# S5 operators on GpSimd in a fixed order, six output buffers, and the output phase's loads behind them

## The chip, the cores and the metric

The kernel runs on one core of one Trainium2 chip. The metric is device microseconds (us) of one execution. Before the change three runs took 2718.73, 2725.08 and 2727.89 us; their median is 2725.08 us.

The engines are named as the profile names them: PE (TensorE), DVE (VectorE), ACT (ScalarE), POOL (GpSimd) and SP (SyncE, which issues DMAs). Each engine works through its own queue in order. An instruction that waits holds up all that stands behind it in that queue, DMA issues among them.

## The reference

A trunk of two layers over a sequence of 1024 tokens of width 1024, in float32: a gated linear attention (GLA) layer, then an S5 layer. In each layer the normalised input goes through one wide projection, whose columns feed the sequence mixer (width 2048), a gate z (3072) and a query (1024) for a cross-attention into 256 memory rows.

```python
for i in range(DEPTH):
    h = rms_norm(x, norm_w[i])
    ...
        seq_out, z, xq = s5_branch(h, s5_w_in[j], s5_lam_re[j], ...)
    xa = memory_attention(xq, mem_n, xa_w_kv[i])
    y = jnp.concatenate([seq_out.astype(x.dtype), xa.astype(x.dtype)], axis=-1) * jax.nn.silu(z)
    x = x + y @ w_out[i]
return rms_norm(x, final_norm_w)
```

The S5 mixer splits the 2048 channels into 128 groups of 16, each with 64 complex states: x_t = A x_{t-1} + B u_t and y_t = Re(C x_t), then a GELU and a gated product with `w_glu`.

## The kernel before

All matrix products go through `gemm` (L86): every float32 weight tile is loaded by SP (`wr`, L78) and split into a high part `wh` (ACT, L69) and a low part `wl` (DVE, L70), and each product is made of three matmuls.

The S5 layer works in steps of 8 tokens. For that it builds three kinds of operator matrices from the parameters, for 16 blocks n of 8 groups each:

- *In-chunk operators* (`s5_operators`, L774 to L821) hold what a token contributes within its own 8 tokens. POOL makes the factors (L785 to L807), ACT copies some of them into `cz`, PE multiplies them (L811), DVE and ACT form a Toeplitz tile (L814, L815), ACT issues seven DMAs that shift it (L818), copies it (L820) and stores it as `tp` in DRAM (L821).
- *Input operators* (`s5_input_operators`, 32 of them) take tokens to states. POOL issues two loads for each, `ib` (L754) and `ipw` (L757), one operator ahead, computes with L767 to L770, and stores `rt` to DRAM (L771).
- *Output operators* (`s5_output_operators`, 32 of them) take states to tokens. POOL multiplies powers `pwo` (loaded once by SP, L719) with parameters `oc` (L728): first multiply L741, second L742, then L743, and the store of `od` to DRAM (L744).

Input and output operators share buffers `op` (three) and `opt` (one) of pool `ip1`. In `run()` the in-chunk operators are called between the output projections of the first layer, all input and output operators before `mem_attention` of the second layer (scores, softmax, product `ps_b` with the values, gate, y at L322, store of y by SP at L323; y has two buffers). Then `s5()` runs.

`s5()` has two parts of eight units. A unit projects `u` (weights `w_su`), stores it to DRAM (L870), loads it in another layout (`uu`, L872) and forms with `rt` the inputs of the states (L853 to L860). A recurrence on DVE (L883, L885, L887) then walks through the 128 steps, in two independent chains per part. The output phase loads per half unit `uq` (L896), `tp` (L898) and `ow` (L900, the stored output operator), copies states into `xg`, and multiplies (L908, L909).

The order of the instructions on each engine is not the order of the calls. The Tile framework's scheduler orders them by a timeline that it simulates, by data dependences and by when buffers come free. Where a pool is closed, a later pool takes over its memory, and the later tiles wait for the last use of the earlier ones. The tiles of `s5()` lie in part in memory of the operators' pool:

```python
tile.TileContext(nc, schedule_with_timeline_sim=True)
...
return ctx.enter_context(self.tc.tile_pool(name=name, bufs=bufs, reuse_waits="tile"))
```

Of the kernel before, what the change touches and what calls it, by code (L numbers as in the profile page):

```python
# [8 lines left out]
F32 = mybir.dt.float32  # L9
# [7 lines left out]
P = 128  # L17
HALF = 512
# [27 lines left out]
class Trunk:  # L46
# [675 lines left out]
    def s5_output_operators(self, pool, powers, ns):  # L722

        nc = self.nc

        def load(n):
            c = pool.tile([P, 2, 4, 16], F32, tag="oc", name="oc", bufs=3)
            nc.gpsimd.dma_start(c.rearrange("p r g h -> p (r g h)"), self.t["s5_par"][n][:, 128:256])  # L728
            return c

        sh = [P, 4, 8, 16]
        nxt = load(ns[0])
        for n in ns:
            c, nxt = nxt, load(n + 1) if n < ns[-1] else None
            pw = [powers[:, i, 4 * n:4 * n + 4].rearrange("p g (d o) -> p g d o", o=1).broadcast_to(sh) for i in range(2)]
            c = [c[:, i].rearrange("p g (o h) -> p g o h", o=1).broadcast_to(sh) for i in range(2)]
            od = self.o_d[n].rearrange("(r p) (i g) x -> r i p g x", r=2, i=2)
            for r, op in enumerate((ALU.subtract, ALU.add)):
                o = pool.tile([P, HALF], F32, tag="op", name="op", bufs=3).rearrange("p (g t h) -> p g t h", g=4, h=16)
                tm = pool.tile([P, HALF], F32, tag="opt", name="opt", bufs=1).rearrange("p (g t h) -> p g t h", g=4, h=16)  # L740
                nc.gpsimd.tensor_tensor(o, pw[0], c[r], ALU.mult)  # L741
                nc.gpsimd.tensor_tensor(tm, pw[1], c[1 - r], ALU.mult)  # L742
                nc.gpsimd.tensor_tensor(o, o, tm, op)  # L743
                nc.gpsimd.dma_start(od[r], o.rearrange("p g t h -> p g (t h)"))  # L744

    def s5_input_operators(self, pool):

# [25 lines left out]
    def s5_operators(self, pool, n):  # L773

        nc, t, v = self.nc, self.t, self.nc.vector
        M, A, S = ALU.mult, ALU.add, ALU.subtract
        gs = slice(4 * n, 4 * n + 4)
        G = 4
        par = pool.tile([P, 448], F32, tag="par", name="par", bufs=2)
        nc.gpsimd.dma_start(par, t["s5_par"][n])  # L780
        view = lambda a, b, pat, **kw: par[:, a:b].rearrange(pat, **kw)
        b = view(0, 128, "p (r g h) -> p r g h", r=2, g=G)
        c = view(128, 320, "p (r g h) -> p r g h", r=3, g=G)
        dd = view(320, 448, "p (i g h) -> p i g h", i=2, g=G)
        nc.gpsimd.tensor_scalar(par[:, 192:320], par[:, 192:320], -1.0, None, M)  # L785
        cz = self.cz[n % 2]
        halves = [slice(64 * i, 64 * i + 64) for i in range(2)]
        for i, hp in enumerate(halves):
            nc.scalar.copy(cz[hp, :, :, 0, i], c[hp, 0:2])
        c4 = pool.tile([P, 2, G, 16], F32, tag="c4", name="c4", bufs=2)  # L790
        l4 = [self.pw[:, i, gs, 4:5].broadcast_to([P, G, 16]) for i in range(2)]
        for i in range(2):
            tm = pool.tile([P, G, 16], F32, tag="ptm", name="ptm", bufs=1)
            nc.gpsimd.tensor_tensor(c4[:, i], l4[0], c[:, i], M)
            nc.gpsimd.tensor_tensor(tm, l4[1], c[:, i + 1], M)
            nc.gpsimd.tensor_tensor(c4[:, i], c4[:, i], tm, A)
        for i, hp in enumerate(halves):
            nc.scalar.copy(cz[hp, :, :, 1, i], c4[hp])
        r = pool.tile([P, 2, G, 4, 16], F32, tag="r", name="r", bufs=2)
        sh = [P, G, 4, 16]  # L800
        pw = [self.ip[:, i, 4:8, gs].rearrange("p s g -> p g s").rearrange("p g (s o) -> p g s o", o=1).broadcast_to(sh) for i in range(2)]
        xs = [b[:, i].rearrange("p g (o h) -> p g o h", o=1).broadcast_to(sh) for i in (0, 1, 1, 0)]
        for i, op in ((0, S), (1, A)):
            tm = pool.tile(sh, F32, tag="ctm", name="ctm", bufs=1)
            nc.gpsimd.tensor_tensor(r[:, i], pw[0], xs[2 * i], M)
            nc.gpsimd.tensor_tensor(tm, pw[1], xs[2 * i + 1], M)
            nc.gpsimd.tensor_tensor(r[:, i], r[:, i], tm, op)  # L807
        pk = self.ps("a")[0:64, :G * 64]
        for g in range(G):
            for ri in range(2):  # L810
                nc.tensor.matmul(pk[:, g * 64:(g + 1) * 64], r[:, ri, g].rearrange("p s h -> p (s h)"), cz[:, ri, g].rearrange("p e i h -> p (e i h)"), start=ri == 0, stop=ri == 1)  # L811
        pk = pk.rearrange("p (g e i h) -> p e i g h", g=G, e=2, i=2)
        tp = self.toep[n % 2]
        v.tensor_tensor(tp[64:P, 7], pk[:, 0], dd[0:64], A)  # L814
        nc.scalar.copy(tp[0:64, 7], pk[:, 1])  # L815
        for s in range(7):
            w = 16 * (s + 1)
            nc.scalar.dma_start(tp[0:w, s], tp[P - w:P, 7])  # L818
        tg = pool.tile([P, 8, 8, 16], F32, tag="tg", name="tg", bufs=1)
        nc.scalar.copy(tg, tp.rearrange("p t i g h -> p (i g) t h"))  # L820
        nc.scalar.dma_start(self.tp_d[n].rearrange("p a b -> p (a b)"), tg.rearrange("p a t h -> p (a t h)"))  # L821
# [15 lines left out]
    EARLY = 8  # L837

    def s5(self, xs, zs_d, y1_d):
        nc, t, v = self.nc, self.t, self.nc.vector  # L840
        ud = [self.dram.tile([8, P, P], F32, name=f"ud{j}") for j in range(16)]
        by_step = [x.rearrange("s (h g) c -> (s h) g c", g=8) for x in ud]
        with ExitStack() as ctx:
            st = [self.pool(ctx, f"st{i}").tile([P, 2, 32, P + 1], F32, name=f"st{i}") for i in range(2)]
            sp = self.tags(ctx, "s5")
            for part in range(2):
                nc.gpsimd.memset(st[part][:, :, :, 0:1], 0.0)
                def states(j, uu):
                    half, jl = divmod(j, 8)
                    hp = slice(64 * half, 64 * half + 64)  # L850
# [37 lines left out]
            for part in range(2):  # L888
                for j in self.PARTS[part]:
                    half, jl = divmod(j, 8)  # L890
                    hp = slice(64 * half, 64 * half + 64)
                    yo = sp.tile([P, 8, P], F32, tag="uy", name="uy", bufs=3)
                    for q in range(2):
                        n, hb = 2 * jl + q, slice(4 * half, 4 * half + 4)
                        uq = sp.tile([P, 4, P], F32, tag="uq", name="uq", bufs=2)
                        nc.sync.dma_start(uq, by_step[j][:, 4 * q:4 * q + 4, :])  # L896
                        tp = sp.tile([P, 4, P], F32, tag="rtp", name="rtp", bufs=3)
                        nc.sync.dma_start(tp, self.tp_d[n][:, hb, :])  # L898
                        ow = sp.tile([P, 4, P], F32, tag="ow", name="ow", bufs=2)
                        nc.sync.dma_start(ow, self.o_d[n][:, hb, :])  # L900
                        xg = sp.tile([P, 4, P], F32, tag="xg", name="xg", bufs=2)
                        g0 = 8 * (jl % 4) + 4 * q
                        nc.scalar.copy(xg[0:64], st[part][hp, 0, g0:g0 + 4, 0:P])
                        nc.vector.tensor_scalar(xg[64:P], st[part][hp, 1, g0:g0 + 4, 0:P], -1.0, None, ALU.mult)
                        ps = self.ps("a")
                        for g in range(4):
                            o = ps[:, g * P:(g + 1) * P]
                            nc.tensor.matmul(o, tp[:, g], uq[:, g], start=True, stop=False)  # L908
                            nc.tensor.matmul(o, ow[:, g], xg[:, g], start=False, stop=True)  # L909
                        nc.scalar.activation(yo[:, 4 * q:4 * q + 4, :], ps.rearrange("p (g c) -> p g c", g=4), AF.Gelu_apprx_tanh)  # L910
                    nc.sync.dma_start(y1_d[j].rearrange("s (h g) c -> (s h) g c", g=8), yo)
# [50 lines left out]
    def run(self):  # L962
        nc, tc, t = self.nc, self.tc, self.t
# [6 lines left out]
        with ExitStack() as ctx:  # L970
# [14 lines left out]
            with ExitStack() as c2:  # L985
# [12 lines left out]
                with ExitStack() as c3:  # L998
                    late, pool = self.pool(c3, "xl0"), self.pool(c3, "xa0")
# [41 lines left out]
            with ExitStack() as c2:  # L1041
                qp = self.pool(c2, "xq1")
                self.kvp = self.pool(c2, "kv1")
                late, pool = self.pool(c2, "xl1"), self.pool(c2, "xa1")
                ip = self.pool(c2, "ip1")
                self.s5_input_operators(ip)
                self.s5_output_operators(ip, self.s5_output_powers(ip), range(16))
                self.mem_attention(qp, late, pool, self.mem_kv_reload, t["w_sx"], [t["w_sz"][16 + i] for i in range(8)], xs1, y_d[1])
            self.s5(xs1, zs_d, y1_d)
            self.glu(xp, y1_d, zs_d, y_d[1])  # L1050
# [95 lines left out]
```

## Time and profile before

| | before |
|---|---|
| median of three runs | 2725.08 us |
| the profiled execution | 2727.05 us |
| its span in the trace | 2725.3 us |
| mean granted TensorE clock | 0.955 of full speed |
| PE busy | 2468.2 us (91%) |
| DVE busy | 1285.9 us (47%) |
| ACT busy | 834.0 us (31%) |
| POOL busy | 597.1 us (22%) |

The page cuts the span into 40 slices of 68 us. The row of PE has 9 in most of them, and 4, 5 and 0 in some of the slices between 1160 and 1700 us; POOL works from slice 14 to slice 24 and hardly anywhere else. The shares are means over stages that are limited by different things, so the stretches are read one by one. The profiled execution lies 2 us above the median.

### The profile page before, as it was taken

How to read it: one execution, taken by the hardware profiler on the slowest of the kernel's cores; microseconds unless marked ns; L12 is line 12 of the kernel's file. 1: busy time of each engine (PE TensorE's matmuls, PEld its weight loads, DVE VectorE, ACT ScalarE, POOL GpSimd, SP SyncE). 2: the span in 40 equal slices, each digit the busy share in tenths (PEclk: the TensorE clock that was granted, in tenths of full speed). 3: DMA queues.
4: the chain of work that ended last, by engine and by line, in shares of the span. 5: the costliest groups of instructions: out<-in, count | busy, mean ns of one | idle time of the engine just before them, and what ended most of it. 6: DMA issues, size and time to landing. Idle time of an engine off the chain costs nothing.

```text
span 2725.3 us, 32666 instructions
## 1 busy us (share of the span) xinstructions
PE 2468.2 (91%) x12000; PEld 2056.0 (75%) x12000; DVE 1285.9 (47%) x3272; ACT 834.0 (31%) x1422; POOL 597.1 (22%) x713
## 2 busy tenths in 40 slices
PE   7999999999999999974599605999999999999998
PEld 6888878888888877753488504888888888888887
DVE  7553354545456343781343200499984222232345
ACT  5422243434344222431222102334225111131243
POOL 6200000000000148988844441000000000000015
PEclk9999999999999999987699857999999999999999
DMA  6512122222223676754423114556859333345434
GB/s 222 182 50 71 55 70 70 70 70 70 70 70 117 219 239 185 242 186 137 147 88 91 41 29 159 169 163 203 276 161 313 130 116 128 131 148 194 154 118 161
DMA packets 206751, 375.58 MB, mean 138 GB/s; under 512 B 36768, under 2 KB 97824, under 8 KB 206592
## 3 DMA queue, kind: packets, MB, share of 16 engines
q1 hardware_dynamic: 165120, 323.01, 36.3%
q0 software_dynamic: 30208, 38.43, 5.2%
q10 hardware_dynamic: 11264, 12.07, 1.3%
q8 instruction: 94, 1.54, 0.2%
q14 instruction: 65, 0.53, 0.1%
HBM read 274.07 MB, written 95.55 MB: 136 GB/s over the span
## 4 chain that ended last, share of the span: by engine, by line
PE 71%; DMA 14%; POOL 5%; DVE 5%; ACT 3%; issue 2%; ACTq 0%; SPq 0%; POOLq 0%; DVEq 0%
PE ps_mm L86 60%; DMA od<-op 9%; PE ps_b L86 2%; PE ps_o L86 1%; POOL op L741 1%; DVE X L70 1%; DMA yr<-y 1%; PE ps_a L856 1%; PE ps_a L909 1%; DMA ipw<-ip_d 1%; DVE wl L70 1%; PE ps_a L908 1%; PE ps_a L86 1%; PE ps_s L86 1%; POOL x L170 1%
## 5 line engine op out<-in xcount | busy, mean ns | idle before, releaser
L86 PE MATMUL ps_mm<-X,wh 128*128 128x512 f32 (+1 forms) x4992 | 1533.4, 388 | 29.2 <-DVE zs L255 10.9
L86 PEld LDWEIGHTS ps_mm<-X,wh 128*128 128x128 f32 x4992 | 932.1, 189 | 219.0 <-ACT wh L69 12.1
L86 PE MATMUL ps_mm<-X,wl 128*128 128x512 f32 (+1 forms) x2496 | 966.5, 387 | 8.7 <-DVE wl L70 8.7
L86 PEld LDWEIGHTS ps_mm<-X,wl 128*128 128x128 f32 x2496 | 472.5, 189 | 105.4 <-DVE wl L70 13.7
L70 DVE TENSOR_TENSOR wl<-wr,wh 128x1024 fp32r<-128x1024 f32 x256 | 341.5, 1334 | 424.8 <-ACT wh L69 365.0
L69 ACT CAST wh<-wr 128x1024 fp32r<-128x1024 f32 x256 | 268.9, 1051 | 664.1 <-PE ps_mm L86 594.7
L127 POOL TENSOR_TENSOR nacc<-nacc,nsq 128x512 f32<-128x512 f32 (+1 forms) x30 | 40.4, 1346 | 986.9 <-ACT nsq L125 986.2
L491 POOL TENSOR_TENSOR rs<-ss,mhalf 128x1 f32<-128x1 f32 x32 | 20.2, 632 | 601.3 <-DVE ss L489 601.3
L883 DVE TENSOR_TENSOR pd<-a,st 128x64 f32<-128x64 f32 x508 | 139.8, 276 | 3.6 <-ACT st L860 1.7
L86 PE MATMUL ps_mm<-wh,X 128*128 128x512 f32 x384 | 125.0, 392 | 0.0
L86 PE MATMUL ps_b<-pth,kvh 128*128 128x512 f32 x32 | 13.2, 414 | 123.0 <-DVE y L322 122.5
L255 DVE SCALAR_TENSOR_TENSOR zs<-zt,ps_mm 128x512 f32<-128x512 f32 x96 | 65.4, 682 | 124.9 <-ACT zt L254 113.5
L254 ACT ACTIVATE zt<-ps_mm 128x512 f32<-128x512 f32 x96 | 57.0, 593 | 185.7 <-PE ps_mm L86 162.3
L887 DVE TENSOR_TENSOR st<-st,pd 128x32 f32<-128x32 f32 x508 | 107.5, 212 | 2.0
L86 PEld LDWEIGHTS ps_b<-pth,kvh 128*128 128x128 f32 x32 | 6.3, 196 | 124.9 <-DVE y L322 122.9
L70 DVE TENSOR_TENSOR X<-yr,X 128x512 fp32r<-128x512 f32 x96 | 75.1, 806 | 49.0 <-ACT X L69 42.9
L885 DVE TENSOR_TENSOR pd<-pd 128x32 f32<-128x32 f32 x508 | 95.3, 188 | 1.9
L322 DVE SCALAR_TENSOR_TENSOR y<-ps_b,zs 128x512 f32<-128x512 f32 x32 | 22.0, 688 | 140.4 <-DMA y<-y 122.6
L86 PEld LDWEIGHTS ps_mm<-wh,X 128*128 128x128 f32 x384 | 72.0, 188 | 15.0
L957 DVE SCALAR_TENSOR_TENSOR sg<-sg,y 128x512 f32<-128x512 f32 x32 | 22.0, 688 | 126.6 <-ACT sg L954 124.2
L69 ACT CAST X<-yr 128x512 fp32r<-128x512 f32 x96 | 58.5, 620 | 69.2 <-DMA yr<-y 51.9
L86 PE MATMUL ps_mm<-wl,X 128*128 128x512 f32 x192 | 75.0, 391 | 0.0
(411 smaller groups left out, 3426.6 us busy)
## 6 DMA issues: line engine op xcount, KB each, us to landing
wr<-in_w_out SPq DMA_DIRECT2D x72, 512.0 KB, 4.4
yr<-y SPq DMA_DIRECT2D x96, 256.0 KB, 4.4
wr<-in_w_gv SPq DMA_DIRECT2D x32, 512.0 KB, 3.7
wr<-in_w_glu SPq DMA_DIRECT2D x32, 512.0 KB, 3.9
wr<-in_w_gz SPq DMA_DIRECT2D x24, 512.0 KB, 3.7
wr<-in_w_sz SPq DMA_DIRECT2D x24, 512.0 KB, 4.3
wr<-in_w_k SPq DMA_DIRECT2D x16, 512.0 KB, 4.2
wr<-in_w_v SPq DMA_DIRECT2D x16, 512.0 KB, 4.4
```

What stands on the lines that cost most here:

```text
L69: nc.scalar.copy(h, src)
L70: (eng or nc.vector).tensor_tensor(l, src, h.bitcast(F32), ALU.subtract)
L86: self.nc.tensor.matmul(out, a, b, start=start, stop=stop, skip_group_check=True)
L127: eng.tensor_tensor(acc[:, :width], acc[:, :width], sq[:, :width], ALU.add)
L170: nc.gpsimd.tensor_tensor(x, x, rbs, ALU.mult)
L254: self.nc.scalar.activation(th, ps, AF.Tanh, scale=0.5)
L255: self.nc.vector.scalar_tensor_tensor(out, th, 1.0, ps, ALU.add, ALU.mult)
L741: nc.gpsimd.tensor_tensor(o, pw[0], c[r], ALU.mult)
L856: nc.tensor.matmul(pw[:, g * P:(g + 1) * P], rt[:, g], uu[:, 4 * q + g], start=True, stop=True)
L883: v.tensor_tensor(x, a2[:, :, :, g], prev, ALU.mult)
L885: v.tensor_tensor(x[:, :, 0, :], x[:, :, 0, :], x[:, :, 1, :], ALU.add)
L887: v.tensor_tensor(st[part][:, :, g, c], st[part][:, :, g, c], x[:, :, 0, :], ALU.add)
```

## The change

1. The output operators get six buffers `op` instead of three (L739).
2. In `run()`, input and output operators are issued inside `tc.issue_after`, behind the last in-chunk instruction of POOL, so that POOL works through all in-chunk operators, then all input, then all output operators. The pool `ip1` becomes two pools, one after the other: `ip1a` for the input operators, `ip1b` for the output operators, which may take over the memory of `ip1a`.
3. In the output phase of `s5()` the loads of `tp` and `ow` are issued by POOL instead of SP, ordered behind the last store of the output operators.
4. The memset of the states' first column goes from POOL to DVE (L847).

```diff
-                o = pool.tile([P, HALF], F32, tag="op", name="op", bufs=3).rearrange("p (g t h) -> p g t h", g=4, h=16)
+                o = pool.tile([P, HALF], F32, tag="op", name="op", bufs=6).rearrange("p (g t h) -> p g t h", g=4, h=16)
...
-                nc.gpsimd.dma_start(od[r], o.rearrange("p g t h -> p g (t h)"))
+                self.made = nc.gpsimd.dma_start(od[r], o.rearrange("p g t h -> p g (t h)"))
...
-            nc.gpsimd.tensor_tensor(r[:, i], r[:, i], tm, op)
+            self.made = nc.gpsimd.tensor_tensor(r[:, i], r[:, i], tm, op)
...
-                nc.gpsimd.memset(st[part][:, :, :, 0:1], 0.0)
+                nc.vector.memset(st[part][:, :, :, 0:1], 0.0)
...
-                        nc.sync.dma_start(tp, self.tp_d[n][:, hb, :])
+                        loads = [nc.gpsimd.dma_start(tp, self.tp_d[n][:, hb, :])]
                         ow = sp.tile([P, 4, P], F32, tag="ow", name="ow", bufs=2)
-                        nc.sync.dma_start(ow, self.o_d[n][:, hb, :])
+                        loads.append(nc.gpsimd.dma_start(ow, self.o_d[n][:, hb, :]))
+                        for x in loads:
+                            tc.add_manual_dep(x.ins, self.made.ins.name, mybir.DependencyInfo(mybir.DependencyClass.NoSync, mybir.DependencyReason.DATA), reason="order")
...
-                ip = self.pool(c2, "ip1")
-                self.s5_input_operators(ip)
-                self.s5_output_operators(ip, self.s5_output_powers(ip), range(16))
+                with tc.issue_after(self.made.ins):
+                    with ExitStack() as c3:
+                        self.s5_input_operators(self.pool(c3, "ip1a"))
+                    with ExitStack() as c3:
+                        ip = self.pool(c3, "ip1b")
+                        self.s5_output_operators(ip, self.s5_output_powers(ip), range(16))
```

The scheduler then orders the queues anew. Three places follow; the rows of a queue stand in the order in which its engine takes them (line, instruction, output<-inputs, shape; numbers behind names tell tiles apart).

**First place: PE, the in-chunk products L811.** Before, around the projection `ps_mm_10303` of the first layer's output, and further on the last in-chunk products (`ps_a_10125` is that of the last block, n = 15), which stood behind the projections `ps_mm_11371` of the second layer:

```order
L86 MATMUL ps_mm_10303<-X_9519,wh_10299 128x512
L86 MATMUL ps_mm_10303<-X_9518,wl_10300 128x512
L86 MATMUL ps_mm_10335<-X_9476,wh_10331 128x512
...
L86 MATMUL ps_mm_11371<-X_10572,wl_11304 128x512
L811 MATMUL ps_a_9813<-cz1_8490,r_9804 64x64 x8
...
L811 MATMUL ps_a_10047<-cz0_8489,r_10038 64x64 x8
L811 MATMUL ps_a_10125<-cz1_8490,r_10116 64x64 x8
L86 MATMUL ps_mm_11400<-X_10544,wh_11309 128x512
```

Now:

```order
L86 MATMUL ps_mm_10303<-X_9519,wh_10299 128x512
L86 MATMUL ps_mm_10303<-X_9518,wl_10300 128x512
L811 MATMUL ps_a_10125<-cz1_8490,r_10116 64x64 x8
L86 MATMUL ps_mm_10335<-X_9476,wh_10331 128x512
L86 MATMUL ps_mm_10335<-X_9477,wh_10331 128x512
```

The last product stands right behind the projection `ps_mm_10303`, ahead of everything of the second layer's projections.

**Second place: POOL, in the output operators.** Before, in the steady state (L741 takes a new buffer `op`, L744 stores one):

```order
L741 TENSOR_TENSOR op_10995<-pwo_10947,oc_10979 128x512
L744 DMA od2_3449<-op_10981 2x64x512
L742 TENSOR_TENSOR opt_10988<-pwo_10947,oc_10965 128x512
L743 TENSOR_TENSOR op_10987<-op_10987,opt_10988 128x512
L728 DMA oc_11007<-in_s5_par 128x128
L741 TENSOR_TENSOR op_11001<-pwo_10947,oc_10979 128x512
L744 DMA od2_3449<-op_10987 2x64x512
L742 TENSOR_TENSOR opt_10996<-pwo_10947,oc_10979 128x512
L743 TENSOR_TENSOR op_10995<-op_10995,opt_10996 128x512
L741 TENSOR_TENSOR op_11009<-pwo_10947,oc_10993 128x512
```

Now:

```order
L741 TENSOR_TENSOR op_11027<-pwo_10951,oc_11011 128x512
L743 TENSOR_TENSOR op_10999<-op_10999,opt_11000 128x512
L741 TENSOR_TENSOR op_11033<-pwo_10951,oc_11011 128x512
L744 DMA od3_3450<-op_10999 2x64x512
L742 TENSOR_TENSOR opt_11006<-pwo_10951,oc_10983 128x512
L743 TENSOR_TENSOR op_11005<-op_11005,opt_11006 128x512
L728 DMA oc_11025<-in_s5_par 128x128
L744 DMA od3_3450<-op_11005 2x64x512
L742 TENSOR_TENSOR opt_11014<-pwo_10951,oc_10997 128x512
L741 TENSOR_TENSOR op_11041<-pwo_10951,oc_11025 128x512
```

Before, one multiply L741 stands between every two stores. Now two multiplies, for the two operators of a block, stand close together, then two stores, with the parameters' load between them.

**Third place: SP, the loads whose memory POOL's operators hold.** Before, ahead of `s5()`, the first loads of the output phase (L900), and further on in the states of unit 4 and 5 (with what each row waits for, by semaphore):

```order
L323 DMA y1_21_123<-y_12550 128x512 [waits DMAHW0_49,DVE_49]
L900 DMA ow_16374<-od0_3447 128x512 [waits DMASW4_49,DMASW3_49,DMASW5_49,DMASW2_49,DMASW6_49,DMASW1_49,DMASW7_49,DMASW0_49,Pool_49]
L900 DMA ow_16396<-od1_3448 128x512 [waits DMASW4_49,DMASW3_49,DMASW6_49,DMASW2_49,DMASW7_49,DMASW1_49,DMAHW2_49,DMASW0_49,Pool_49]
L78 DMA wr_13267<-in_w_su 128x1024 [waits DMAHW3_49,DVE_49]
...
L872 DMA uu_14767<-ud4_13014 128x1024 [waits DMAHW7_49]
L870 DMA ud5_13015<-uy_14769 128x8x128 [waits DMAHW1_49,Activation_49]
L78 DMA wr_15170<-in_w_su 128x1024 [waits DMAHW2_49,DVE_49]
```

Now, at the states of the same units:

```order
L78 DMA wr_15094<-in_w_su 128x1024 [waits DVE_49]
L872 DMA uu_14771<-ud4_13018 128x1024 [waits DMAHW1_49]
L896 DMA uq_16371<-ud0_13014 128x512 [waits DMAHW5_49,Pool_49]
L896 DMA uq_16396<-ud0_13014 128x512 [waits DMASW6_49,DMASW5_49,DMASW7_49,DMASW4_49,DMAHW6_49,DMASW1_49,DMASW0_49]
L870 DMA ud5_13019<-uy_14773 128x8x128 [waits DMAHW7_49,Activation_49]
L853 DMA rtp_14924<-rt11_3426 128x512 [waits DMAHW0_49,PE_49]
L78 DMA wr_15174<-in_w_su 128x1024 [waits DVE_49]
```

`ow` is gone from SP. The first two loads of `uq` (L896), which stood at the first unit, now stand ahead of the store `ud5`, and the first of them waits for a count of POOL that the last output operator's second multiply (L742) reaches.

## Rows read from the trace of the kernel before

**Rows 1.** stretches: us, busy PE, PEld, DVE, ACT, POOL, PEclk, DMA, GB/s

```profile
1227.00:1350.00 123.00, 51.31 (x259) 41.53 (x260) 25.39 (x30) 25.38 (x48) 107.79 (x151) 0.65 0.50 154
1541.00:1664.00 123.00, 1.46 (x6) 0.86 (x5) 0.78 (x2) 0.00 (x0) 52.80 (x52) 0.52 0.19 52
1770.00:1870.00 100.00, 100.00 (x507) 85.17 (x506) 99.60 (x620) 37.88 (x59) 0.00 (x0) 1.00 0.52 164
```

**Rows 2.** TensorE's waits, whole program: us in all, times, longest us

```profile
PE ps_b L86 <- DVE y L322: 122.7, 2, 122.5
...
PE ps_a L811 <- POOL ctm L806: 44.6, 3, 16.3
...
PE ps_a L811 <- POOL c L796: 13.4, 1, 13.4
...
PE ps_mm L86 <- DVE zs L255: 10.9, 1, 10.9
```

**Rows 3.** what SP's DMA queue waited for, the same columns

```profile
SPq L900 <- DMA od<-op: 154.1, 2, 136.3
```

**Rows 4.** SP's timeline around its wait: start us, us, instruction, out<-in

```profile
1486.08 0.33 SPq L323 DMA_DIRECT2D y<-y  x1
...
1499.53 0.32 SPq L900 DMA_DIRECT2D ow<-od  x1
...
1654.23 0.32 SPq L900 DMA_DIRECT2D ow<-od  x1
```

**Rows 5.** POOL's instructions by form: busy us, mean ns, idle before

```profile
L767 POOL TENSOR_TENSOR op<-ipw,ib 128x512 f32<-128x512 f32 x32 | 41.8, 1307 | 18.8 <-DMA ipw<-ip_d 16.3 <-DMA ib<-in_s_b 2.5
...
L741 POOL TENSOR_TENSOR op<-pwo,oc 128x512 f32<-128x512 f32 x32 | 36.2, 1132 | 148.7 <-DMA od<-op 148.3 <-DMA rt<-op 0.4
...
L770 POOL TENSOR_TENSOR op<-op,opt 128x256 f32<-128x256 f32 x32 | 28.4, 887 | 0.0
```

**Rows 6.** timeline of TensorE at the in-chunk place and at the S5 states

```profile
1157.59 0.39 PE L86 MATMUL ps_mm<-X,wl 128*128 128x512 f32 x1
...
1788.37 1.95 PE L856 MATMUL ps_a<-uu,rtp 128*128 128x128 f32 x16
```

**Rows 7.** POOL's timeline, last input operators; in brackets the idle before

```profile
1318.56 1.26 POOL L767 TENSOR_TENSOR op<-ipw,ib 128x512 f32<-128x512 f32 x1 [2.50 <-DMA ib<-in_s_b]
...
1326.91 1.26 POOL L767 TENSOR_TENSOR op<-ipw,ib 128x512 f32<-128x512 f32 x1 [2.69 <-DMA ipw<-ip_d]
...
1328.81 0.73 POOL L770 TENSOR_TENSOR op<-op,opt 128x256 f32<-128x256 f32 x1
...
1334.25 1.72 POOL L770 TENSOR_TENSOR op<-op,opt 128x256 f32<-128x256 f32 x1
```

**Rows 8.** timeline of POOL in the output operators

```profile
1553.30 0.84 POOL L744 DMA_DIRECT2D od<-op  x1
...
1557.17 0.82 POOL L744 DMA_DIRECT2D od<-op  x1
...
1562.28 1.10 POOL L741 TENSOR_TENSOR op<-pwo,oc 128x512 f32<-128x512 f32 x1 [3.15 <-DMA od<-op]
...
1567.14 0.84 POOL L744 DMA_DIRECT2D od<-op  x1
...
1640.87 0.83 POOL L744 DMA_DIRECT2D od<-op  x1 [0.30 <-POOL op L743]
...
1644.48 0.83 POOL L744 DMA_DIRECT2D od<-op  x1 [0.30 <-POOL op L743]
```

**Rows 9.** timeline of SP's queue in the S5 phase

```profile
1772.19 0.32 SPq L872 DMA_DIRECT2D uu<-ud  x1
```

**Rows 10.** timeline of VectorE in the S5 recurrence

```profile
1767.04 0.28 DVE L883 TENSOR_TENSOR pd<-a,st 128x64 f32<-128x64 f32 x1
```

**Rows 11.** tile kvh, 1200 to 1345: ns min/median/max, first and last start

```profile
L70 DVE TENSOR_TENSOR kvl<-wr,kvh x4: 1224/1752/3369, 1330.3 to 1339.3; 128x1024 fp32r<-128x1024 f32 x4
```

**Rows 12.** ScalarE's waits, 990 to 1160: us in all, times, longest us

```profile
ACT tg L820 <- DMA toep<-toep: 25.2, 5, 9.8
```

More of the change, by code (lines that the diff above doesn't have):

```diff
@@ L839, in s5 @@
     def s5(self, xs, zs_d, y1_d):
-        nc, t, v = self.nc, self.t, self.nc.vector
+        nc, t, v, tc = self.nc, self.t, self.nc.vector, self.tc
         ud = [self.dram.tile([8, P, P], F32, name=f"ud{j}") for j in range(16)]
```

## The prediction

> **What bounds the kernel now.** I read the stretches first: busy time, clock and DMA share of each. TensorE works nearly all the time except in two places. From 1227 to 1350 us it is busy for 51 of 123 us, from 1541 to 1664 for 1.5 of 123 us [rows 1]. The list of what TensorE waited for then names the causes [rows 2]: the in-chunk products L811 waited 44.6 + 13.4 us for POOL, and the projections 10.9 us for VectorE's gate behind them, 69 us in all. The second gap is one wait of 122.5 us for VectorE's y (L322).
>
> VectorE's y was not late by its own work. The waits of SP's queue show one load of `ow` (L900) held for the stores of the output operators, 154.1 us in two waits [rows 3], and SP's timeline shows the place: it comes to L900 at 1499.53 and its next issue is at 1654.23 [rows 4]. `ow` lies in the memory of the operators' pool. Behind it stood three weight loads and the stores of y; the two y buffers filled, and TensorE stopped at 1541.
>
> So POOL's own chain sets both gaps: first the in-chunk and input operators mixed, then 32 output operators, in which L741 waits 148.3 us in 29 waits for the store that still reads its buffer [rows 5].
>
> **The change, part by part.** I follow POOL, since everything that may hold the program now waits for it.
>
> *In-chunk first.* In TensorE's queue the last in-chunk product now stands right behind the projection that ended in the trace at about 1158 (first place quoted above; [rows 6]). I let POOL start the input operators at 1160. The earliest is 1158; the latest is 1316, where in the trace the input operators get POOL for themselves [rows 7]. I take the early end because POOL no longer mixes other work in, and give it 25 us of doubt.
>
> *Input operators.* Left to themselves, one took 1326.91 - 1318.56 = 8.35 us, the waits for its loads included [rows 7]. On the program's mean L767 is 0.05 longer than there (1.31 against 1.26), L770 and its twin L769 some 0.16 each (0.89 against 0.73) [rows 5, 7], so about 8.75; 32 x 8.75 = 280, and 5 us for the first loads (of which [rows 7] show the unhidden half, 2.5 to 2.7). End: 1160 + 5 + 280 = 1445. Ends of the range: 8.35 (267 in all) and 11.35 (363), the slow ones next to a kv split, below.
>
> *The powers' load.* The second pool inherits the memory of the first, so L719 on SP, which stands where the y stores of the trace's 1486 stand, waits for the last input operator. SP would come there 69 us earlier than in the trace [rows 4], at 1417, and stay until about 1441. Behind it stand a y store and w_su loads; VectorE has a second y buffer, so TensorE may lose 10 us of these 24. This costs nothing in the sum as long as POOL arrives later still at the next point. The load lands about when POOL ends its last input operator: 0.
>
> *Output operators with six buffers.* POOL's order is now one multiply and store, then a second pair of these, with the multiplies that need the next two buffers between them (second place quoted above). The trace of before holds one such pair by chance: stores at 1553.30 and 1557.17, the waiting L741 from 1562.28, the next store at 1567.14 [rows 8]. The first store gave its buffer back after 9.0 us although the second ran beside it, and the pair took 13.84 us. An operator without a wait takes 3.6 us from store to store (1640.87 to 1644.48, [rows 8]). First pair: six multiplies L741 of 1.13 [rows 5] + 2 x 3.6 = 14; 26 of the 32 operators still wait, 13 pairs x 13.84 = 180; the last two pairs 4 x 3.6 = 14, less 2 from the end of the last second multiply L742 to the last store. Sum 206. That multiply is done at 1445 + 206 = 1651.
>
> *The loads on POOL.* 64 issues leave SP; on POOL they cost at most 64 x 0.84, a store's issue [rows 8], 54 us in a stretch of over 200 in which it has nothing else to do. On SP the wait of 154.1 us goes. The Trainium skill ("DMA: Bandwidth & Descriptors", section "Issuing engines are not separate DMA queues") holds that moving a DMA to another issuing engine saves only the sequencer's time to start it; by that alone the move would give nothing and the forecast would stay at 2725. The trace shows something that the rule doesn't speak of [rows 3, 4]: what is saved is the place behind a wait in an engine's order, not the issue.
>
> *What is late next.* Two new waits point at POOL's last second multiply, because tiles of the S5 phase (`uq`, `pd`) lie in memory that the output operators use now. SP stops at the first `uq` (L896), right behind the `uu` load that it issued at 1772.19 (third place quoted above; [rows 9]), and VectorE at the second step of the recurrence's second chain (L883), which it passed at 1767.04 [rows 10]. Behind SP stand the ud store and uu load for TensorE's states that the trace has at 1788.37 [rows 6]; behind VectorE the rest of a recurrence in which it is busy 99.6 of 100 us [rows 1], so that no delay there is made up. With both gaps gone VectorE's place would come at 1767 - 122.5 - 69 = 1575; POOL says 1651. VectorE thus runs 1767 - 1651 = 116 us ahead of before. TensorE restarts some 10 us after POOL's release, 1788 - 1661 = 127 ahead, and soon waits for VectorE; the tail behind is as it was.
>
> *The memset of the states* moves to VectorE: two instructions no larger than the 0.28 us one of the same width [rows 10], ahead of that same wait, so 0. Without that cover it is 0.6.
>
> Sum, against the profiled execution's own 2727.05: 2727 - 116 = 2611. The median of the runs is 2 us lower, so I forecast **2609**.
>
> **The rivals.**
> *A, nothing new binds:* POOL would be through by 1575. Time 2727 - 122.5 - 69 = 2535. For it: the new waits stand more than 100 us behind POOL's old end. Against it: from 1158, even 5 + 32 x 8.35 + 206 ends at 1636.
>
> *B, POOL is slowed by VectorE.* At 1334 L770 took 1.72 us against 0.73 five us before [rows 7], while VectorE split the kv weights, in up to 3.37 us against 1.22 at the least [rows 11]. The input operators now run beside attention. If three of their multiplies and adds are each 1.0 longer throughout, one takes 11.35; POOL ends at 1160 + 5 + 363 + 206 = 1734, time 2727 - 33 = 2694, median 2692. Against: only four such splits stand there, and beside attention L741 kept its 1.13 [rows 5]. The Trainium skill ("SBUF — State Buffer", section "SBUF: two separate sides") states such a rule: VectorE with two SBUF inputs and GpSimd reading SBUF lock one another out for a whole instruction. The trace agrees with it in that place [rows 7, 11].
>
> *C, the six buffers do not do what they say.* If stores still went one at a time, each operator costs a return of 9.0 and a multiply, about 9.9, and the phase 32 x 9.9 = 317; POOL ends at 1762, time 2722: no change. Against: [rows 8].
>
> *D, slower.* The in-chunk operators come as late as before, because not POOL's load but their own path sets their pace: POOL, ScalarE, TensorE, VectorE, seven DMAs and back. Between 990 and 1160 ScalarE waited 25.2 us in five waits for these DMAs [rows 12]. Then POOL has all 32 input operators still ahead of it at 1316: 1316 + 5 + 280 + 206 = 1807, 40 us later than VectorE came to that place, time 2767. It decides from an in-chunk end of 1284 on, where POOL is 8 us beyond 1767. Against: 5 us per wait fit into a step of about 12, and two operators are in flight.
>
> *E, the output phase waits for POOL's loads,* which now stand in one order behind one another: 32 steps at one or two us each, 2640 to 2670.
>
> **How the numbers follow.** The forecast gets 0.66, with a range of its own of 2585 to 2640 (input operators of 8.35 to 9.2 us, start at 1158 to 1185, pairs of 13.8 to 14.6). A 0.04, B 0.14, C 0.05, D 0.06, E 0.05. The range reaches down to 2580, where POOL is quick at every step, and up to 2690, which takes in E and nearly all of B; A, C and D lie outside. 0.3% is 8 us, about what a measurement can tell from no change. Faster: the forecast, A, B and E, 0.89; same: C, 0.05; slower: D, 0.06.
>
> **What would show it.** In the profile after: no wait of SP on `ow`; L811 no longer waiting for POOL; input operators 8 to 9 us apart from 1160 on; output stores in pairs 14 us apart, the last near 1654; SP and VectorE both waiting for POOL there, and TensorE idle for some 40 to 50 us shortly before 1660, at a low clock. Wrong would be: no such idle time (A), POOL's multiplies at 2 us (B), stores 10 us apart (C), in-chunk products still arriving at 1250 and later (D), TensorE waiting for `rtp` or `ow` in the output phase's products (E).

## The result and the profile after

The changed kernel takes 2625.95 us (median of four runs, 2623.28 to 2633.01). The kernel before, run beside it, takes 2723.11. The ratio is 0.9647 with an interval of 0.962 to 0.9673. The forecast of 2609 was 17 us too low; the measured time lies inside the narrower range given with it. The profiled execution of the changed kernel was the longest of its four, 2633.01 us with a span of 2631.1; the terms below are compared with that one.

TensorE's waits in the profile after, the view of [rows 2] (us in all, times, longest us):

```profile
PE ps_a L856 <- DMA uu<-ud: 71.1, 7, 42.9
...
PE ps_o L145 <- DVE ndg L143: 14.6, 2, 13.1
PE ps_a L811 <- issue: 14.1, 3, 8.8
...
PE ps_a L910 <- DMA uq<-ud: 7.0, 2, 3.7
```

The 122.5 us at y are gone. The in-chunk products' waits for POOL [rows 2] are down to 0.6 us; 14.1 us before them are left for which the profile names no releaser (issue). In place of both TensorE waits for `uu`, the input of the S5 states. The waits of SP's queue and of VectorE say why; SP's wait on `ow` [rows 3] is not there any more:

```profile
SPq L896 <- POOL opt L742: 45.5, 1, 45.5
```

```profile
DVE pd L883 <- POOL opt L742: 39.8, 1, 39.8
```

Both end with POOL's last second multiply. POOL's timeline, from its first input operator to that multiply:

```profile
1173.53 1.27 POOL L767 TENSOR_TENSOR op<-ipw,ib 128x512 f32<-128x512 f32 x1 [6.41 <-DMA ipw<-ip_d]
...
1437.89 0.57 POOL L771 DMA_DIRECT2D rt<-op  x1 [0.30 <-POOL op L770]
1438.45 1.60 POOL L728 DMA_DIRECT2D oc<-in_s_par  x3
1444.59 1.10 POOL L741 TENSOR_TENSOR op<-pwo,oc 128x512 f32<-128x512 f32 x1 [4.54 <-DMA oc<-in_s_par]
...
1458.66 0.84 POOL L744 DMA_DIRECT2D od<-op  x1
...
1643.69 0.84 POOL L744 DMA_DIRECT2D od<-op  x1 [0.31 <-POOL op L743]
...
1661.95 1.12 POOL L742 TENSOR_TENSOR opt<-pwo,oc 128x512 f32<-128x512 f32 x1
```

VectorE, SP and TensorE in their timelines at that place:

```profile
1663.10 0.27 DVE L883 TENSOR_TENSOR pd<-a,st 128x64 f32<-128x64 f32 x1 [39.85 <-POOL opt L742]
```

```profile
1663.09 1.27 SPq L896 DMA_DIRECT2D uq<-ud  x2
...
1674.52 0.32 SPq L872 DMA_DIRECT2D uu<-ud  x1
```

```profile
1682.19 3.75 PE L856 MATMUL ps_a<-uu,rtp 128*128 128x128 f32 x16 [42.93 <-DMA uu<-ud]
```

The multiply ends at 1663.07; within 0.03 us VectorE and SP go on, and 19 us later TensorE. The gap that stood at 1541 to 1664 has shrunk to 1639 to 1682. In the stretches (columns of [rows 1]) the first two lines are the places of [rows 1] in the kernel after, and the third is the new gap, with a granted clock of 0.54, near the lower of the two levels:

```profile
1227.00:1350.00 123.00, 110.63 (x520) 91.72 (x521) 63.26 (x101) 37.06 (x72) 97.58 (x106) 0.92 0.49 152
1541.00:1664.00 123.00, 78.58 (x364) 65.04 (x362) 54.08 (x101) 25.49 (x40) 86.23 (x85) 0.83 0.44 128
...
1639.00:1682.00 43.00, 0.25 (x2) 0.00 (x0) 18.90 (x117) 1.14 (x2) 24.28 (x25) 0.54 0.42 122
```

POOL's groups that answer to [rows 5]:

```profile
L767 POOL TENSOR_TENSOR op<-ipw,ib 128x512 f32<-128x512 f32 x32 | 46.1, 1440 | 66.7 <-DMA ipw<-ip_d 59.3 <-issue 7.3
...
L741 POOL TENSOR_TENSOR op<-pwo,oc 128x512 f32<-128x512 f32 x32 | 36.9, 1159 | 72.1 <-DMA oc<-in_s_par 46.2 <-DMA od<-op 25.8
...
L770 POOL TENSOR_TENSOR op<-op,opt 128x256 f32<-128x256 f32 x32 | 26.1, 817 | 0.0
```

POOL's wait for its own stores fell from 148.3 to 25.8 us. A wait of 46.2 us for the small parameter loads `oc` came up instead.

**How far ahead TensorE is.** I number TensorE's products into `ps_mm` (9,408 in each trace) and compare the starts of the same number before and after. After the first place TensorE is 66 us ahead, behind the second 189, behind the waits for `uu` 104, at the end of the output phase 95, and there it stays. Below, "ahead" is this number. The output phase's products, L908 and L909 before, are L910 and L911 in the changed kernel.

### The profile page after: what moved, and what is told of

It is laid out like the page before. It is cut to its first block, busy times and chain, and to the rows that moved or that the text cites. A ratio compares the mean times of both kernels' runs of the same rounds, so it can differ in the third digit from the quotient of the medians.

```text
span 2631.1 us, 32704 instructions
## 1 busy us (share of the span) xinstructions
PE 2474.5 (94%) x12000; PEld 2061.0 (78%) x12000; DVE 1290.8 (49%) x3274; ACT 834.9 (32%) x1422; POOL 643.1 (24%) x775
## 4 chain that ended last, share of the span: by engine, by line
PE 62%; DMA 15%; POOL 12%; DVE 4%; issue 4%; ACT 3%; POOLq 0%; SPq 0%; DVEq 0%; ACTq 0%
PE ps_mm L86 53%; DMA ipw<-ip_d 5%; DMA od<-op 4%; PE ps_b L86 2%; POOL op L767 2%; DMA yr<-y 1%; PE ps_o L86 1%; DMA par<-in_s_par 1%; POOL op L769 1%; DVE pd L883 1%; POOL op L770 1%; POOL op L741 1%; POOL op L743 1%; PE ps_a L86 1%; DVE wl L70 1%
## 5 line engine op out<-in xcount | busy, mean ns | idle before, releaser
L883 DVE TENSOR_TENSOR pd<-a,st 128x64 f32<-128x64 f32 x508 | 145.2, 286 | 45.2 <-POOL opt L742 39.8
L887 DVE TENSOR_TENSOR st<-st,pd 128x32 f32<-128x32 f32 x508 | 117.5, 232 | 2.2
L885 DVE TENSOR_TENSOR pd<-pd 128x32 f32<-128x32 f32 x508 | 106.1, 209 | 2.1
L856 PE MATMUL ps_a<-uu,rtp 128*128 128x128 f32 x256 | 38.4, 313 | 71.9 <-DMA uu<-ud 71.1
L856 PEld LDWEIGHTS ps_a<-uu,rtp 128*128 128x128 f32 x256 | 36.7, 225 | 76.0 <-issue 62.1
L70 DVE TENSOR_TENSOR X<-yr,X 128x512 fp32r<-128x512 f32 x96 | 66.9, 716 | 56.1 <-ACT X L69 50.1
L898 POOL DMA_DIRECT2D rtp<-tp x32 | 17.4, 544 | 279.0 <-PE ps_a L911 188.5
```

What stands on the lines that cost most here:

```text
L70: (eng or nc.vector).tensor_tensor(l, src, h.bitcast(F32), ALU.subtract)
L856: nc.tensor.matmul(pw[:, g * P:(g + 1) * P], rt[:, g], uu[:, 4 * q + g], start=True, stop=True)
L883: v.tensor_tensor(x, a2[:, :, :, g], prev, ALU.mult)
L885: v.tensor_tensor(x[:, :, 0, :], x[:, :, 0, :], x[:, :, 1, :], ALU.add)
L887: v.tensor_tensor(st[part][:, :, g, c], st[part][:, :, g, c], x[:, :, 0, :], ALU.add)
```

## The experiments

Each kernel is compared with runs of before on the same chip. The medians of before in the four sets are 2723.11 (beside the change), 2726.96, 2728.86 and 2726.01, so medians of different sets compare to some 6 us, and differences taken by the ratios are given beside them where that matters. The theory: with SP's wait at `ow` gone, POOL's last L742 sets the end, one for one. The main rival: the gain came from moving the loads off SP.

**Three buffers instead of six** (`e1_bufs3`).

```diff
-                o = pool.tile([P, HALF], F32, tag="op", name="op", bufs=6)...
+                o = pool.tile([P, HALF], F32, tag="op", name="op", bufs=3)...
```

> Only undoes the six buffers (three again), all else as changed. Theory (POOL's last output operator releases SP and VectorE, and every us of its chain counts one for one): the output operators take some 9.7 us each as before, 310 us instead of 225, POOL ends near 1748, and the time is 2626 + 85 = 2711. Rival (the parameter loads, not the buffers, pace the operators): 2626 to 2640.

2665.74 us, ratio 0.9776 (0.9756 to 0.9796): 40 us slower than the change (35 by the ratios), not 85. In its trace POOL's wait for its stores is 100.4 us, and SP's wait for the last L742 doubles:

```profile
L741 POOL TENSOR_TENSOR op<-pwo,oc 128x512 f32<-128x512 f32 x32 | 37.4, 1169 | 105.6 <-DMA od<-op 100.4 <-DMA oc<-in_s_par 5.2
```

```profile
SPq L896 <- POOL opt L742: 97.8, 1, 97.8
```

The last L742 starts at 1694.1, 32 us later than with six, and TensorE ends 59 us ahead instead of 94, 35 less. One for one holds. My size was off because it left out that with three buffers POOL hardly waits for `oc`: 74.6 more for the stores, 41.0 less for `oc`.

**The loads of `tp` and `ow` back on SP, at the same late place** (`e2_loads_sp`): `nc.gpsimd.dma_start` becomes `nc.sync.dma_start` in L898 and L900, with the order behind POOL's stores kept.

> Only puts the loads of tp and ow back on SP, still ordered behind the last store. In SP's order ow then stands right behind the first uq. Theory (what counts is where the waiting load stands and when POOL ends, not which engine issues it): SP waits some 8 to 11 us longer, for the landing of the last stores instead of the last multiply, 2634 to 2640. Rival (taking the loads off SP is what closed the gap of 122 us): 2626 + 110 = 2736.

2619.78, ratio 0.9608 (0.9587 to 0.963): no slower than the change. SP waits only 8.4 us at `ow`, and TensorE's waits for `uq` fall from 7.0 to 0.8 us:

```profile
SPq L900 <- DMA od<-op: 8.4, 1, 8.4
```

```profile
PE ps_a L910 <- DMA uq<-ud: 0.8, 1, 0.8
```

TensorE keeps what it has behind the gap (110 ahead, 109.5 at the end), where the change loses 9. So issuing on POOL isn't what closed the gap; a late place in the order does as well on SP. That rival falls.

**Without the fixed order** (`e3_no_order`), the operators where the scheduler puts them:

```diff
-                with tc.issue_after(self.made.ins):
+                with ExitStack():
```

> Only undoes the fixed order: input and output operators may again mix with the in-chunk ones; six buffers, two pools and loads on POOL stay. Theory: POOL ends its input operators near 1340 as before instead of 1438 and its output operators near 1570, so the second gap goes and nothing waits for POOL behind it, while the first gap of 69 us stays: 2727 - 122 + 10 = 2610 to 2620. Rival (the order is worth the first gap in full): 2626 + 69 = 2695.

2642.66, ratio 0.9681 (0.966 to 0.9703): 17 us slower than the change by the medians, 9 by the ratios, whose intervals overlap. It is clear of `e5_memset` below, a kernel as fast as the change in the same set (0.9611 to 0.9647), by 15 us. The first gap is back:

```profile
PE ps_a L811 <- POOL ctm L806: 44.9, 3, 17.0
PE ps_a L856 <- DMA uu<-ud: 28.8, 2, 21.2
...
PE ps_a L811 <- POOL c L796: 13.1, 1, 13.1
```

But POOL's input operators run from 1001.8 and its last L742 starts at 1568.1, 94 us earlier than in the change, so the wait for `uu` falls from 71.1 to 28.8. Closing the first gap gives 66 us, and most of it is paid back at the second, since POOL's end moves out: behind it TensorE is 97 ahead here and 104 in the change. The profiled execution took 2633.27 here, 9 us under the median, and 2633.01 in the change, 7 over it, so the two traces end level.

**The memset back on POOL** (`e5_memset`).

> Only puts the memset of the states back on POOL, where it now stands between the output operators. Theory: POOL comes there near 1500, when attention has just released that memory, 0 to 10 us: 2624 to 2636. Rival (it holds POOL as it did before, 23 us): 2650.

2627.52, ratio 0.9629 (0.9611 to 0.9647): no difference. Its last L742 starts at 1651.5, and in `e2_loads_sp` at 1655.0: with the same operators on POOL, its chain differs by up to 10 us between the profiled executions, and that of the change, 1661.95, is the late one.

**One wait taken away at a time.** A tile of 64 columns that nothing uses moves `pd` out of the operators' memory, so that VectorE's wait goes (`v1_pad`). The `uq` loads on POOL behind its stores take SP's wait away (`v2_uq`). Then both (`v3_both`).

```diff
+                pad = self.pool(c2, "pad").tile([P, 64], F32, name="pad")
+                nc.vector.memset(pad[:, 0:1], 0.0)
...
-                        nc.sync.dma_start(uq, by_step[j][:, 4 * q:4 * q + 4, :])
+                        loads = [nc.gpsimd.dma_start(uq, by_step[j][:, 4 * q:4 * q + 4, :])]
```

> Lays a small unused tile under the operators' pool, so that the recurrence's tiles pd no longer lie in its memory: VectorE's wait for POOL goes, SP's at the first uq stays. Theory (either of the two waits holds the program alone): TensorE stops at the same states, 2615 to 2630. Rival (VectorE's wait alone holds it): 2626 - 60 = 2566.

> Issues the loads of uq on POOL too: SP's wait goes, VectorE's at pd stays. Theory (either of the two holds the program alone): VectorE still starts its second chain near 1660 and TensorE runs out of split weights a little later, 2610 to 2635. Rival (SP's wait alone holds it): 2626 - 60 = 2566.

> Takes both waits away (unused tile under the pool, uq on POOL). Theory with a port shared by VectorE and POOL: TensorE passes the states 172 us ahead of before, but the recurrence runs beside POOL's output operators until about 1663 and its steps take about 2.2 times as long there (1.49 against 0.69 us, as in the profile after), which costs some 34 us; with 10 us for the loads on POOL 2590 to 2600. Rival (the recurrence runs at its full speed there): 2560 to 2570.

2628.85 (ratio 0.9645, 0.9616 to 0.9674) and 2634.97 (0.9658, 0.9641 to 0.9675). The one wait that is left, of SP in `v1_pad` and of VectorE in `v2_uq`:

```profile
SPq L896 <- POOL opt L742: 45.2, 1, 45.2
```

```profile
DVE pd L883 <- POOL opt L742: 34.9, 1, 34.9
```

Either wait alone is enough, as the theory says. Both taken away give 2613.56 (0.9571, 0.954 to 0.9601), 12 us better than the change by the medians (21 by the ratios) and not the 26 to 36 expected. Without the waits, VectorE runs its recurrence beside POOL's output operators, and each step is slow there. Its groups, first beside POOL (1560 to 1665), then behind it (1665 to 1800):

```profile
L883 DVE TENSOR_TENSOR pd<-a,st 128x64 f32<-128x64 f32 x76 | 34.7, 483 | 7.5 <-ACT st L860 6.7
L885 DVE TENSOR_TENSOR pd<-pd 128x32 f32<-128x32 f32 x76 | 30.3, 422 | 0.9
L887 DVE TENSOR_TENSOR st<-st,pd 128x32 f32<-128x32 f32 x76 | 27.1, 388 | 0.9
...
L883 DVE TENSOR_TENSOR pd<-a,st 128x64 f32<-128x64 f32 x256 | 59.2, 272 | 0.1
L887 DVE TENSOR_TENSOR st<-st,pd 128x32 f32<-128x32 f32 x254 | 42.9, 213 | 0.1
L885 DVE TENSOR_TENSOR pd<-pd 128x32 f32<-128x32 f32 x256 | 39.8, 189 | 0.2
```

That is (483 - 272) + (422 - 189) + (388 - 213) = 619 ns more for each of 76 steps, 47 of the 105 us. SP's load of the next weights (L78) waits 22.6 us and is let go at 1666 by one of these instructions; the next `uu` load stands behind it, and TensorE waits 25.2 us for that. So POOL holds VectorE back by its work as well as by its memory.

**POOL faster, at three places.** Input loads two ahead instead of one, with three buffers each (`v5a_in`; in the kernels with this edit the lines behind it are 2 higher):

> Loads for the input operators two operators ahead instead of one (three buffers each), all else as changed. Theory (POOL's chain counts one for one): an input operator takes 6.3 us instead of 8.05, POOL ends 56 us earlier, near 1607, and the time is 2565 to 2575. Rival (the waits at POOL's end are not what holds the program): 2620 to 2630.

2617.44 (0.96, 0.9576 to 0.9625): 42 us or more above the theory, nearer to the rival. The input operators gained their 56 us (the last `rt` store is issued at 1382.14 instead of 1437.89), and POOL then stood still:

```profile
POOL op L741 <- DMA oc<-in_s_par: 50.5, 13, 5.6
POOL op L741 <- DMA pwo<-pw_d: 35.8, 1, 35.8
```

```profile
1415.06 0.38 SPq L719 DMA_DIRECT2D pwo<-pw_d  x1
```

The load of the powers stands in SP's order behind weight loads and a y store that keep TensorE's pace, so it goes out at 1415 however early POOL is done. The last L742 comes 18 us earlier, and TensorE ends 14 us further ahead: one for one again.

With that load issued by POOL right behind its last input operator (`v5b_in_pwo`: `nc.gpsimd` for `nc.sync` in L719):

> Input operators loaded two ahead, and the load of the output powers (pwo) issued by POOL right behind its last input operator instead of by SyncE. In v5a_in POOL's input operators ended at 1379 us, 59 us earlier than in the changed kernel, but the pwo load was issued only at 1415.06, so POOL's output operators ended only 18 us earlier. Theory (POOL's end sets the end one for one, and pwo's place on SyncE held it back): the output operators keep their 225 us from the last input operator on, POOL ends at about 1379 + 225 = 1604, VectorE resumes 163 us ahead of the kernel before, some 10 to 15 us are lost in the output phase: 2568 to 2585 us. Rival (another wait takes pwo's place, or VectorE beside POOL is slower for the whole gain): 2605 us or more.

2597.3 (0.9521, 0.9496 to 0.9547), between the two theories. The last L742 starts at 1610.2 and so ends 7 us later than expected. VectorE no longer waits for POOL, but its first 15 steps there run beside it at 821, 499 and 576 ns, and TensorE still waits 32.1 us for `uu` and loses 20 in the output phase (144 ahead, then 124). Here one for one no longer holds: 52 us on the last L742 gave 40 behind the gap and 29 at the end.

The stores of the output operators, written on 128 rows of one piece each (`v7_store`, the change with this alone, the loads of `ow` from the new layout):

```diff
-            od = self.o_d[n].rearrange("(r p) (i g) x -> r i p g x", r=2, i=2)
+            od = self.o_d[n].rearrange("(r q) c x -> r q (c x)", r=2)
...
-                self.made = nc.gpsimd.dma_start(od[r], o.rearrange("p g t h -> p g (t h)"))
+                self.made = nc.gpsimd.dma_start(od[r].rearrange("q (h x) -> (q h) x", h=2), o.rearrange("p g t h -> p (g t h)"))
...
-                        loads.append(nc.gpsimd.dma_start(ow, self.o_d[n][:, hb, :]))
+                        loads.append(nc.gpsimd.dma_start(ow, self.o_d[n].rearrange("p c x -> (p c x)").rearrange("(r i p g x) -> i r p g x", r=2, i=2, p=64, g=4)[half]))
```

> The changed kernel with the 32 output stores and the loads of ow written on 128 rows of one contiguous piece each, instead of the form with two halves of the column index outermost; the order of operations is the same. Theory (the landing of the old form, 9.1 us, sets part of the 14.8 us of a pair of output operators): pairs of 12 to 13 us, POOL's output operators end 30 to 40 us earlier, 2585 to 2605 us. Rival (a pair is set by POOL's own work and the loads of oc, and the stores land beside it): pairs stay at 14 us or more, 2615 to 2630 us.

2645.49 (0.9698, 0.9676 to 0.9719): 20 us slower than the change (14 by the ratios), outside the ranges of theory and rival alike. POOL did even better than the theory: last L742 at 1594.6, 67 us earlier, TensorE's wait for `uu` 27.0, 161 us ahead. Then the output phase lost 82 of them, down to 79. The list of DMA issues (KB of one, median us to landing) of the change, then of this kernel, and this kernel's wait:

```profile
od<-op POOLq DMA_DIRECT2D x32, 256.0 KB, 9.6
...
ow<-od POOLq DMA_DIRECT2D x32, 256.0 KB, 6.4
```

```profile
od<-op POOLq DMA_DIRECT2D x32, 256.0 KB, 3.2
ow<-od POOLq DMA_DIRECT2D x32, 256.0 KB, 11.2
```

```profile
PE ps_a L911 <- DMA ow<-od: 35.6, 10, 5.6
```

The slow form has moved from the store to the load. TensorE waits 35.6 us for `ow` itself; between 1700 and 2030 it stands idle for 57 of 330 us at a granted clock of 0.89, and in the change for 9 at 0.99.

```profile
1700.00:2030.00 330.00, 273.14 (x1336) 232.55 (x1335) 205.55 (x977) 89.81 (x147) 43.20 (x61) 0.89 0.59 177
```

All of it (`v9_all`): `v5b_in_pwo`, the 128-row stores, and `tp` and `ow` on SP, each `ow` as two loads of 64 rows, meant to leave the slow form on neither side:

```diff
+                        loads += [nc.sync.dma_start(ow[64 * r:64 * r + 64], self.o_d[n].rearrange("p c x -> (p c x)").rearrange("(r i p g x) -> i r p g x", r=2, i=2, p=64, g=4)[half][r]) for r in range(2)]
```

> v5b_in_pwo with the 128-row stores of v7_store, and with the loads of tp and ow back on SyncE. Theory: the gains add as far as TensorE has room: POOL ends at about 1570 us, the lead at VectorE's release is 172 to 180 us instead of 107, and the output phase gives little of it back: 2548 to 2565 us. Rival (recurrence operations of VectorE that now stand beside POOL's output operators are slowed, and give it back, as in v3_both): 2585 us or more.

2542.81 (0.932, 0.9294 to 0.9346), 83 us below the change and 5 below the theory's range. The store lands in 2.7 us, a half of `ow` in 4.7. The last L742 starts at 1541.5, ahead of the recurrence, which begins at 1549. VectorE's groups (1545 to 1650) and the stretches:

```profile
L885 DVE TENSOR_TENSOR pd<-a,st 128x64 f32<-128x64 f32 x180 | 43.4, 274 | 3.9 <-ACT st L862 2.6 <-DVE st L889 0.3
L889 DVE TENSOR_TENSOR st<-st,pd 128x32 f32<-128x32 f32 x178 | 31.8, 214 | 1.1
L887 DVE TENSOR_TENSOR pd<-pd 128x32 f32<-128x32 f32 x180 | 29.3, 189 | 1.2
```

```profile
1390.00:1545.00 155.00, 153.43 (x769) 129.36 (x768) 51.23 (x83) 45.81 (x90) 141.18 (x141) 1.00 0.51 172
1545.00:1645.00 100.00, 100.00 (x507) 85.20 (x506) 91.25 (x520) 34.68 (x56) 0.00 (x0) 1.00 0.57 182
```

TensorE is busy for 253.4 of 255 us, at a granted clock of 1.00, and no wait for `uu` is left there. It is 193 us ahead, 184 at the end.

One load of all `oc` up front and four buffers (`v8_oc`):

> v9_all with one load of all output parameters (oc) ahead of the output operators in place of 16 loads, and four buffers of the output operators instead of six. Theory: POOL ends some 20 to 40 us before v9_all's; if that was still what VectorE waited for, 2545 to 2555 us, and if TensorE's own work sets the pace by then, the same time as v9_all within 6 us. Rival (the four buffers come free too late): slower than v9_all by over 10 us.

2537.14 (0.9293, 0.926 to 0.9327). The last second multiply (L743 there) starts at 1533.7, 8 us earlier than in `v9_all`, not 20 or more. The time is within 6 us of it and the intervals overlap. In both kernels VectorE and TensorE no longer wait for POOL's end, and SP 0.2 us at most.

## Why the prediction was right

*What bounds it, and the two new waits:* right. The wait on `ow` went, SP and VectorE stop at `uq` and `pd` for POOL's last L742, and TensorE stands idle shortly before POOL's end, at a low clock. `v1_pad` and `v2_uq` show that either wait holds the program, `e1_bufs3` and `v5a_in` that TensorE's place behind the gap moves with POOL's end, later and earlier. TensorE restarted 19 us behind POOL's release and not 10, so SP's wait alone put it 1788.37 - 1682.19 = 106 us ahead, about where VectorE's put it, which fits either being enough.

*The terms,* in the profiled execution:

| step | predicted | profile after |
|---|---|---|
| first input operator | 1160 | 1173.5 |
| one input operator | 8.75 | 264.9 / 32 = 8.3 |
| last input operator done | 1445 | 1438 |
| a pair of output operators | 13.84 | 185.0 / 12.5 = 14.8 |
| last L742 done | 1651 | 1663.1 |
| VectorE at L883 ahead | 116 | 1767.04 - 1663.10 = 103.9 |
| kernel ahead at the end | 116 | 2727.05 - 2633.01 = 94.0 |

POOL was done with the in-chunk work at 1167.1, 7 us later than taken, and then waited 6.4 for the first loads, for which the sum had 5 behind the start. Quicker operators gave this back, and the last was done 7 us early. That these two errors pull against each other is luck: the start was 8 us late with that wait counted, and the 32 operators took 15 us less than the 280. Of the 19 us that the output phase is over its 206, 6 stand ahead of its first multiply, the three `oc` loads and the wait for them, and some 1 us in each pair: it now waits for `oc` more than for the store, which the fragment of before [rows 8] couldn't show. That a second store in flight hardly slows the first was right: the stores land in 9.6 us at the median, and in 9.1 in the kernel before, which mostly has one at a time. In the runs with the same operators on POOL (`e2_loads_sp`, `e5_memset`, `v1_pad`, `v2_uq`) the last L742 starts at 1651.5 to 1655.0, so some 9 of these 12 us are that execution's.

*Rival E* was right that loads on POOL cost the output phase something, and small: that phase gives 9 us back in the change and none in `e2_loads_sp`. Its sign, waits for `rtp` or `ow`, did not come (0.7 us at `ow`). TensorE waits 7.0 us for `uq`, which SP loads, and how the loads on POOL bring that about isn't shown. The prediction priced it as a case by itself, where it belonged into the sum. These are the two mis-sized terms: POOL's end 12 us late and the output phase 9.5 us worse, 2611 + 12 + 9.5 = 2633 for the profiled execution. The prediction weighed a rule of the Trainium skill ("DMA: Bandwidth & Descriptors", section "Issuing engines are not separate DMA queues"): issuing DMAs from several engines at once saves only the sequencer's time to start them. `e2_loads_sp` agrees, 2619.78 on SP against 2625.95 on POOL. What the change saved was the place in the order.

*Rival B* priced the right mechanism at the wrong place. POOL's input operators were hardly slowed (L767 at 1440 ns against 1307, L770 at 817 against 887, one operator at 8.3 us), but VectorE's recurrence was. The timelines of both engines in the changed kernel, between 1618 and 1622, show it one by one:

```profile
1618.71 1.10 POOL L741 TENSOR_TENSOR op<-pwo,oc 128x512 f32<-128x512 f32 x1 [3.29 <-DMA oc<-in_s_par]
1619.77 1.26 POOL L743 TENSOR_TENSOR op<-op,opt 128x512 f32<-128x512 f32 x1
```

```profile
1618.46 0.27 DVE L883 TENSOR_TENSOR pd<-a,st 128x64 f32<-128x64 f32 x1
1618.77 1.09 DVE L885 TENSOR_TENSOR pd<-pd 128x32 f32<-128x32 f32 x1
1619.89 1.21 DVE L887 TENSOR_TENSOR st<-st,pd 128x32 f32<-128x32 f32 x1
1621.13 0.27 DVE L883 TENSOR_TENSOR pd<-a,st 128x64 f32<-128x64 f32 x1
1621.44 0.19 DVE L885 TENSOR_TENSOR pd<-pd 128x32 f32<-128x32 f32 x1
```

An L885 of 0.19 us lasts until POOL's multiply ends, the L887 behind it until POOL's next one ends, and once POOL is idle they are short again. The Trainium skill ("SBUF — State Buffer", section "SBUF: two separate sides") states an exclusive lock, held for a whole instruction, between VectorE with two SBUF inputs and GpSimd reading SBUF. These rows agree. It cost the change little, as VectorE had to wait for POOL anyway.

*Rivals A, C and D* did not come: there is a gap at L856; a pair takes 14.8 us, not two times 9.9; POOL was done with the in-chunk work at 1167 and not at 1250 or later, and the in-chunk products no longer wait for its ctm.

*Where the gain came from.* Of the 97 us, 40 go when the six buffers alone are undone (`e1_bufs3`; 35 by the ratios) and 17 when the order alone is (`e3_no_order`; 9 by the ratios); undoing the loads' engine or the memset loses nothing. The remaining 40 or more need not be one part's: with the order taken away or three buffers, SP no longer stands at `ow` either, and a kernel with `ow` at its early place and all else changed was not tried.

## What to carry to other kernels

When a helper engine's chain holds the program through memory that a later phase takes over, find the last instruction that reads that memory and count back from it: here 32 us on that instruction were 35 at the end in one direction, and 18 were 14 in the other, as long as nothing behind it got slower. Look at both sides of a DRAM round trip before a layout is changed, since `v7_store` gained 67 us on POOL and lost more in the output phase, whose loads had become the slow ones. And of a fixed order ask first whether another queue's load (`pwo` on SP) has a place that doesn't move with it.

## What was not expected of the hardware

- The same 256 KB on POOL's queue landed in 9.6 us as a store whose DRAM side has an outermost dimension of 2, and in 3.2 us (2.7 in `v9_all`) on 128 rows; as a load 11.2 us with that dimension and 6.4 without. The Trainium skill ("DMA: Bandwidth & Descriptors", section "Why a DMA increments its semaphore by 16 and not by 1") says that a DMA runs on the largest number of engines, up to 16, that divides the slowest dimensions of both sides. By that the slow form has 2 engines. The packet records of the traces agree: in a store of the kernel before with no other transfer on its queue (issued at 1461.81) the 64 packets of 4 KB take 0.208 us each and 6.93 us together, 1.9 at a time on average; in one of `v9_all` (issued at 1443.82), 0.159 us each and 0.78 us together, 13 at a time.
- VectorE's three recurrence instructions, 272, 189 and 213 ns by themselves, were 483, 422 and 388 ns beside POOL's output operators in `v3_both`.
